# Softmax probabilities divided at the attention output, the table add fused with the row maximum, and the output projection's weight splits moved to GpSimd

## The chip, the cores and the metric

The kernel runs on one core of one Trainium2 chip. Five engines work in parallel, each through its own queue in order: TensorE (PE in the profile, with its weight loads shown apart as PEld), VectorE (DVE), ScalarE (ACT), GpSimd (POOL) and SyncE (SP), which here issues every transfer between the chip's memory (HBM) and the on-chip buffer (SBUF). TensorE writes only into PSUM, eight banks of 128 x 512 float32. The metric is the device time of one execution in microseconds (us); lower is better.

## The reference, cut to what matters

The program is two layers of a diffusion backbone over 256 latent tokens of width 1024, with 256 context tokens beside them in the first layer. Each layer is a half-step feed-forward, a mixer, and a second half-step feed-forward, each followed by a layer norm. The mixer of layer 0 is the neighbourhood attention that the change touches: 16 heads of 64, each latent query sees the latent keys in a window of 16 columns (a position table is added to these scores, and masked keys get minus infinity) and all 256 context keys, in one softmax.

```python
s_win = jnp.einsum('bjqhd,bjkhd->bhjqk', q_r, k_blk).astype(jnp.float32) * scale
s_win = jnp.where(mask, s_win + bias.astype(jnp.float32)[None], -jnp.inf)
s_ctx = jnp.einsum('bjqhd,bchd->bhjqc', q_r, k_c).astype(jnp.float32) * scale
p = jax.nn.softmax(jnp.concatenate([s_win, s_ctx], axis=-1), axis=-1).astype(v.dtype)
return (jnp.einsum('bhjqk,bjkhd->bjqhd', p[..., :nk], v_blk)
        + jnp.einsum('bhjqc,bchd->bjqhd', p[..., nk:], v_c))
...
y_lat = jnp.moveaxis(o, 0, 1).reshape(B, S, D) @ w_out
```

All matrices are float32, and the products have to keep nearly float32 precision.

## The kernel before, in words

**Precision.** TensorE multiplies in a rounded float32 type. Every operand x is therefore split into hi (x rounded, made by ACT with a copy) and lo (x minus hi, made by DVE with a subtraction), and each product is three matmuls: hi by hi, hi by lo, lo by hi (function `mmu`, lines 156, 157 and 159). Weights go through `wunit`: SP loads a unit of 128 x 1024 into one of four raw buffers, ACT makes hi (line 178), DVE makes lo (line 181). Activations go through `split` (lines 105 and 106).

**Order.** TensorE's instructions stand in the order in which the Python code issues them. For the other engines a scheduler chooses the order by priority; `tc.high_priority(offset=n)` lets what stands under it go ahead of the n instructions issued before it. For weight units n is `W_EARLY` = 40.

**The attention stage** is one loop over 32 steps. A step is one head h and one half qt of the 256 queries (128 queries), in the order (h,0), (h+1,0), (h,1), (h+1,1), so that two steps share a pair of heads. What one turn i of the loop issues:

- in even turns, `scores` for steps i and i+1: six matmuls into two PSUM banks S (128 queries x 512 keys: 256 latent, then 256 context; line 814). Then for each bank DVE adds the table to the 256 latent scores (818) and takes the negated row maximum over all 512 (820), ACT takes exp with that as bias and sums the row (822), DVE inverts the sum (823), and ACT multiplies the row by the inverse (824). The result is the tile pr.
- `bias_pair` for the pair of steps two turns ahead: SP gathers the table for each head from HBM, POOL adds the window mask (line 730). The table comes reversed within each grid row of 64 keys, and line 818 reads it backwards.
- `probs_T` for step i-2: four TensorE transposes of pr into a PSUM bank (line 836), then a split into pT (hi by ACT, lo by DVE).
- `values` for a head whose second half is done, one turn later: eight matmuls with v (lines 848 and 849) into a bank, then ACT and DVE (854, 855) add the two halves of the bank into `osum`, which holds two heads, and after the odd head `split` turns `osum` into oT, the operand of the output projection.
- between these, `fill_some` issues fillers: groups of six 512-column matmuls of the coming q, k and v projections (wkv, wq) and, from turn 24 on, of the output projection (wo, in `last_filler`). How many a turn gets is set by the table `rate` (R0 to R3). From turn 24 on it is one a turn, until nine are out; the other seven follow the loop.

Transposes of k (kT, line 773), of q and of pr share two PSUM banks (tag "tp"), so each waits until ACT and DVE have split what the bank held before. After the stage follow the layer norm and the second feed-forward.

## Time and profile before

| quantity | value |
|---|---|
| median of 3 runs | 1286.15 us (1283.31 to 1291.49) |
| the profiled execution: own time | 1289.17 us |
| its span, first to last instruction | 1287.4 us |
| instructions | 17193 |
| TensorE busy | 1257.7 us (98%) |
| VectorE busy | 955.1 us (74%) |
| ScalarE busy | 591.2 us (46%) |
| GpSimd busy | 42.0 us (3%) |
| mean granted TensorE clock | 0.996 |
| HBM traffic | 268.59 MB, mean 209 GB/s |

The durations that follow all come from the one profiled execution. A row of a group names the line, the engine, the operation, output and inputs, the shape and the count; behind the bar stand the total busy time, the mean of one in ns, and how long the engine stood idle just before, with what ended the idleness. TensorE's matmuls are pipelined and their ends are modelled: a 512-column matmul is shown with 390 ns, but the next one starts 227 ns later, so a busy TensorE can hold small gaps.

### The profile page before, as it was taken

What the parts mean: (1) busy time and instruction counts of PE and PEld (TensorE: products, weight loads), DVE (VectorE), ACT (ScalarE), POOL (GpSimd) and SP (SyncE); (2) the same over time, 40 slices, a digit from 0 to 9 for tenths busy, and PEclk for the clock granted to TensorE, in tenths of its full rate; (3) what the DMA queues carried; (4) which work ended last, traced back from release to release, by engine and by line L of the source; (5) the groups of instructions that cost most, each with busy time, mean ns of one, the idle gap of its engine ahead of it and who ended that gap; (6) DMA issues with size and microseconds to landing.
All of it is one profiled execution on the core that took longest, in us unless ns stands there. A gap on an engine that the chain in (4) does not pass through costs nothing.

```text
span 1287.4 us, 17193 instructions
## 1 busy us (share of the span) xinstructions
PE 1257.7 (98%) x5890; PEld 1007.0 (78%) x5890; DVE 955.1 (74%) x1683; ACT 591.2 (46%) x1148; POOL 42.0 (3%) x71
## 2 busy tenths in 40 slices
PE   7999999999999999988999999999999999999997
PEld 4787778788778877766887787887787877788886
DVE  3699877485658777788998787757778788855545
ACT  2432132413236456686555435654435645655431
POOL 0000000000001111110000000000000000000000
PEclk9999999999999999999999999999999999999999
DMA  9977569484622744464999887666887764666641
GB/s 284 299 231 243 181 193 297 131 297 146 198 78 76 215 91 92 90 147 149 305 331 328 295 294 262 215 215 225 289 287 241 215 211 147 210 217 185 231 155 51
DMA packets 202712, 268.59 MB, mean 209 GB/s; under 512 B 30026, under 2 KB 149298, under 8 KB 202624
## 3 DMA queue, kind: packets, MB, share of 16 engines
q1 hardware_dynamic: 202624, 267.49, 65.9%
q8 instruction: 46, 0.75, 0.2%
q14 instruction: 42, 0.34, 0.1%
HBM read 265.27 MB, written 2.17 MB: 208 GB/s over the span
## 4 chain that ended last, share of the span: by engine, by line
PE 78%; DVE 8%; DMA 8%; ACT 3%; issue 2%; SPq 1%; POOL 0%; DVEq 0%; ACTq 0%
PE w L156 13%; PE w L157 13%; PE w L159 13%; PE f L541 6%; PE f L542 6%; PE f L543 6%; DMA ar<-in_ada_w_dram 5%; DMA w1r<-in_ffn_w_in_dram 2%; PE wkv L156 2%; PE wkv L157 2%; PE wkv L159 2%; PE wc L156 2%; PE wc L157 2%; PE wc L159 2%; DVE w1l L181 2%
## 5 line engine op out<-in xcount | busy, mean ns | idle before, releaser
L178 ACT ACTIVATE w1h<-w1r 128x512 fp32r<-128x512 f32 x352 | 203.3, 626 | 185.0 <-PE w L159 75.4
L181 DVE TENSOR_TENSOR w1l<-w1r,w1h 128x512 fp32r<-128x512 f32 x352 | 227.6, 684 | 66.5 <-ACT w1h L178 64.3
L156 PE MATMUL w<-w1h,hTh 128*128 128x512 f32 x528 | 211.6, 401 | 3.8 <-ACT hTh L105 3.7
L247 DVE SCALAR_TENSOR_TENSOR acc<-ar,cst,acc 128x512 f32<-128x512 f32 x266 | 187.2, 745 | 34.8 <-DMA ar<-in_ada_w_dram 34.8
L157 PE MATMUL w<-w1l,hTh 128*128 128x512 f32 x528 | 207.7, 393 | 0.0
L156 PE MATMUL w<-w2h,gh 128*128 128x512 f32 (+1 forms) x446 | 175.4, 394 | 0.0
L157 PE MATMUL w<-w2l,gh 128*128 128x512 f32 (+1 forms) x446 | 173.7, 390 | 0.3 <-DVE w2l L181 0.3
L178 ACT ACTIVATE w2h<-w2r 128x512 fp32r<-128x512 f32 x176 | 101.5, 624 | 140.9 <-PE w L159 131.6
L159 PE MATMUL w<-w1h,hTl 128*128 128x512 f32 x528 | 163.9, 392 | 0.6 <-DVE hTl L106 0.6
L181 DVE TENSOR_TENSOR w2l<-w2r,w2h 128x512 fp32r<-128x512 f32 x176 | 114.0, 686 | 43.5 <-ACT w2h L178 42.3
L541 PE MATMUL f<-h0h,w1h 128*128 128x512 f32 x352 | 139.8, 397 | 0.4 <-ACT w1h L178 0.4
L542 PE MATMUL f<-h0h,w1l 128*128 128x512 f32 x352 | 138.4, 393 | 0.0
L543 PE MATMUL f<-h0l,w1h 128*128 128x512 f32 x352 | 138.3, 393 | 0.0
L159 PE MATMUL w<-w2h,gl 128*128 128x512 f32 (+1 forms) x446 | 136.3, 387 | 0.0
L156 PEld LDWEIGHTS w<-w1h,hTh 128*128 128x128 f32 x528 | 99.5, 188 | 28.2 <-ACT hTh L105 5.5
L159 PEld LDWEIGHTS w<-w1h,hTl 128*128 128x128 f32 x528 | 99.5, 189 | 24.1 <-DVE hTl L106 1.4
L157 PEld LDWEIGHTS w<-w1l,hTh 128*128 128x128 f32 x528 | 99.6, 189 | 20.4 <-DVE w1l L181 0.3
L156 PEld LDWEIGHTS w<-w2h,gh 128*128 128x128 f32 x446 | 83.7, 188 | 21.7 <-issue 1.7
L157 PEld LDWEIGHTS w<-w2l,gh 128*128 128x128 f32 x446 | 83.8, 188 | 18.6 <-DVE w2l L181 1.3
L159 PEld LDWEIGHTS w<-w2h,gl 128*128 128x128 f32 x446 | 83.3, 188 | 18.7
L541 PEld LDWEIGHTS f<-h0h,w1h 128*128 128x128 f32 x352 | 66.6, 189 | 18.4 <-issue 3.7
L543 PEld LDWEIGHTS f<-h0l,w1h 128*128 128x128 f32 x352 | 66.5, 189 | 14.7 <-DVE h0l L519 0.3
(178 smaller groups left out, 1702.5 us busy)
## 6 DMA issues: line engine op xcount, KB each, us to landing
w1r<-in_ffn_w_in_dram SPq DMA_DIRECT2D x352, 256.0 KB
ar<-in_ada_w_dram SPq DMA_DIRECT2D x128, 512.0 KB
w2r<-in_ffn_w_out_dram SPq DMA_DIRECT2D x88, 512.0 KB
ar<-in_ada_w_dram SPq DMA_DIRECT2D x32, 256.0 KB
wkvr<-in_na_w_qkv_dram SPq DMA_DIRECT2D x32, 256.0 KB
wcr<-in_sc_w_in_dram SPq DMA_DIRECT2D x32, 256.0 KB
wqr<-in_na_w_qkv_dram SPq DMA_DIRECT2D x8, 512.0 KB
bias<-in_na_rpb_dram SPq DMA_DIRECT2D x64, 64.0 KB
```

Source lines behind the costliest of these rows:

```text
L156: nc.tensor.matmul(ps, lh, rh, start=first and i == 0, stop=False)
L157: nc.tensor.matmul(ps, lh, rl, start=False, stop=False)
L159: nc.tensor.matmul(ps, ll, rh, start=False, stop=last and i == n - 1)
L178: nc.scalar.activation(hi[:, a:a + m // W_HI], raw[:, a:a + m // W_HI], AF.Copy)
L181: nc.vector.tensor_tensor(out=lo[:, a:b], in0=raw[:, a:b], in1=hi[:, a:b].bitcast(F32), op=ALU.subtract)
L247: nc.vector.scalar_tensor_tensor(out=a, in0=src, scalar=sc, in1=a, op0=ALU.mult, op1=ALU.add)
L541: nc.tensor.matmul(ps, lh, hT0[k][0], start=(k == 0), stop=False)
L542: nc.tensor.matmul(ps, ll, hT0[k][0], start=False, stop=False)
L543: nc.tensor.matmul(ps, lh, hT0[k][1], start=False, stop=(k == KC - 1))
```

## The change

Seven edits, all but one in the attention stage:

1. The table add, the maximum over 512 keys and the negation become one DVE instruction, `tensor_tensor_reduce`. It writes S = -(S + table) and the row minimum of that; exp is taken of -S. The table tile now has five slots of 256 columns; the slot in the middle is zero, and each head's operand is its own slot followed by the zero slot, so that all 512 keys can be read as one operand.
2. The reversal of the table moves: k is transposed and split into reversed order within each 64 keys (function `back`), and ACT writes exp back in normal order.
3. The probabilities are no longer divided (the ACT multiplication of line 824 goes). DVE writes the inverse of the row sum 64 times over (128 x 128 for a pair of heads), TensorE transposes that into the free half of the odd head's output bank (two transposes for each pair of heads), and DVE multiplies `osum` by it before the split.
4. In `last_filler`, a flag `calm` changes `wunit`: hi is one ACT instruction of 1024 columns, lo is made by POOL in two of 512, and both get a priority lead of `CALM` = 10 in place of 40. The load keeps its lead of 40.
5. The rate of turns 24 to 31 falls from 1.0 to `R4` = 0.75; turns 32 and on have 1.0. So six fillers go out by turn 31, and one each in turns 32, 33 and 34.
6. The k scratch tiles of 256 columns have five buffers in place of eight.
7. Two small tiles at the start and in the convolution stage (crow, srow) share the two buffers of another small tile (mrow) in place of having their own.

```diff
+CALM = 10
+R4 = 0.75
...
         with tc.high_priority(offset=w_early[0]):
             for src, c in srcs:
                 sync.dma_start(rv[:, :, c:c + src.shape[2]], src)
-            m = kn * 512
+        m = kn * 512
+        if calm[0]:
+            with tc.high_priority(offset=CALM):
+                nc.scalar.activation(hi[:, :m], raw[:, :m], AF.Copy)
+                for a in range(0, m, 512):
+                    nc.gpsimd.tensor_tensor(out=lo[:, a:a + 512], in0=raw[:, a:a + 512],
+                                            in1=hi[:, a:a + 512].bitcast(F32), op=ALU.subtract)
+            return hv, lv
+        with tc.high_priority(offset=w_early[0]):
...
-    crow = cp.tile([16, P], F32, tag="crow", name="crow")
+    crow = sp.tile([32, P], F32, tag="mrow", bufs=2, name="crow")[0:16]
...
-            return hp.tile([P, n], F32, tag="kr", bufs=8, name=nm("kr"))
+            return hp.tile([P, n], F32, tag="kr", bufs=5, name=nm("kr"))
...
+    def back(t):
+
+        return t.rearrange("p (a b) -> p a b", b=64)[:, :, ::-1]
...
+        if not bz:
+            bz.append(hp.tile([P, 5, 4, 64], F32, tag="bias", name="bias"))
+            nc.gpsimd.memset(bz[0][:, 2], 0.0)
         for hh in (h, h + 1):
-            bt = hp.tile([P, 4, 64], F32, tag="bias", bufs=4, name=nm("bias"))
+            n = 3 * qt + hh % 2
+            bt = bz[0][:, n]
...
-            BIAS[hh, qt] = bt[:, :, ::-1]
+            BIAS[hh, qt] = bass.AP(bz[0].tensor, bt.offset, [bt.ap[0], [(2 - n) * 256, 2], [1, 256]])
...
-                split(ps, hi, lo)
+                split(ps.rearrange("p (a b) -> p a b", b=64), back(hi), back(lo))
                 kT.append((hi, lo))
...
+        mx = hp.tile([P, 4 + P], F32, tag="mx", bufs=5, name=nm("mx"))
         for i, S in enumerate(banks):
-            Sv = S[:, 0:256].rearrange("p (a b) -> p a b", a=4)
-            nc.vector.tensor_tensor(out=Sv, in0=Sv, in1=BIAS.pop((h + i, qt)), op=ALU.add)
-            mx = hp.tile([P, 3], F32, tag="mx", bufs=6, name=nm("mx"))
-            nc.vector.tensor_reduce(out=mx[:, 0:1], in_=S, axis=AX.X, op=ALU.max, negate=True)
+            Sv = S.rearrange("p (c n) -> p c n", c=2)
+            nc.vector.tensor_tensor_reduce(out=Sv, in0=Sv, in1=BIAS.pop((h + i, qt)), scale=-1.0, scalar=3.0e38,
+                                           op0=ALU.add, op1=ALU.min, accum_out=mx[:, i:i + 1])
             pr = hp.tile([P, 512], F32, tag="pr", bufs=4, name=nm("pr"))
-            nc.scalar.activation(pr, S, AF.Exp, bias=mx[:, 0:1], accum_out=mx[:, 1:2])
-            nc.vector.reciprocal(mx[:, 2:3], mx[:, 1:2])
-            nc.scalar.activation(pr, pr, AF.Copy, scale=mx[:, 2:3])
+            nc.scalar.activation(back(pr), S.rearrange("p (a b) -> p a b", b=64), AF.Exp, bias=mx[:, i:i + 1], scale=-1.0,
+                                 accum_out=mx[:, 2 + i:3 + i])
             res.append(pr)
+        nc.vector.reciprocal(mx[:, 4:].rearrange("p (i d) -> p i d", i=2), mx[:, 2:4].unsqueeze(2).to_broadcast([P, 2, 64]))
+        RS[h, qt] = mx[:, 4:]
...
-        ps = mmb("o")[:, 0:256]
+        bk = mmb("o")
+        ps = bk[:, 0:256]
+        if h % 2:
+            for qt in range(2):
+                nc.tensor.transpose(bk[:, 256 + qt * P:256 + (qt + 1) * P], RS.pop((h - 1, qt)), ident)
...
+            nc.vector.tensor_tensor(out=osum[0], in0=osum[0], in1=bk[:, 256:512], op=ALU.mult)
             split(osum[0], *(z[:, cs] for z in oT[h // 4]))
...
     def last_filler():
+        calm[0] = True
...
-    rate = [R0] * 8 + [R1] * 8 + [R2] * 8 + [R3] * 12
+    rate = [R0] * 8 + [R1] * 8 + [R2] * 8 + [R4] * 8 + [R3] * 4
...
     run(fill)
     run(fin)
+    calm[0] = False
...
-    srow = cp.tile([24, P], F32, tag="srow", name="srow")
+    srow = sp.tile([32, P], F32, tag="mrow", bufs=2, name="srow")[0:24]
```

What this does to the order of instructions shows best at three places. The first is the end of the attention loop on TensorE, its last two `probs_T` and what follows. Before, the last filler ends, and the transposes of the last two probability tiles (PT) stand back to back with the value products (o) of the last even head right behind them:

```order
L159 MATMUL wo_5288<-woh_5357,oT_5036 128x512 x2
L836 MATMUL PT_5423<-ident,pr_5338 128x128 x4
L836 MATMUL PT_5430<-ident,pr_5345 128x128 x4
L848 MATMUL o_5437<-pT_5370,v_4682 128x256
L849 MATMUL o_5437<-pT_5371,v_4682 128x256
```

In the change the same place on TensorE has a filler of six matmuls between the two, and the product starts behind the second:

```order
L858 MATMUL PT_5293<-ident,pr_5225 128x128 x4
L159 MATMUL wo_5131<-woh_5301,oT_4953 128x512
L160 MATMUL wo_5131<-wol_5302,oT_4953 128x512
L159 MATMUL wo_5131<-woh_5301,oT_4953 128x512
L160 MATMUL wo_5131<-wol_5302,oT_4953 128x512
L162 MATMUL wo_5131<-woh_5301,oT_4954 128x512 x2
L858 MATMUL PT_5313<-ident,pr_5228 128x128 x4
L875 MATMUL o_5320<-pT_5231,v_4624 128x256
L876 MATMUL o_5320<-pT_5232,v_4624 128x256
```

A second such filler now stands between the last even and the last odd head, and behind it, ahead of the odd head's eight products, the two transposes of the inverses (mx):

```order
L160 MATMUL wo_5189<-wol_5282,oT_4953 128x512
L162 MATMUL wo_5189<-woh_5281,oT_4954 128x512 x2
L871 MATMUL o_5338<-ident,mx_5155 128x128
L871 MATMUL o_5338<-ident,mx_5223 128x128
L875 MATMUL o_5338<-pT_5264,v_4624 128x256
```

So three of the nine fillers that the loop hands out have moved from turns 24 to 31 into its last three turns.

The second place is DVE's queue in the last third of the loop, from one pair of steps to the next. Before, it holds for each pair two adds, two reductions, two reciprocals, two pT splits, one `osum` add per head, and the output projection's lo parts (wol):

```order
L181 TENSOR_TENSOR wol_5358<-wor_5356,woh_5357 128x512
L106 TENSOR_TENSOR pT_5016<-PT_5128,pT_5015 128x4x128
L823 RECIPROCAL mx_5075<-mx_5075 128x1
L820 TENSOR_REDUCE mx_5082<-S_5067 128x1
L106 TENSOR_TENSOR pT_5040<-PT_5149,pT_5039 128x4x128
L181 TENSOR_TENSOR wol_5358<-wor_5356,woh_5357 128x512
L855 TENSOR_TENSOR osum_5165<-o_5156,osum_5165 64x256
L823 RECIPROCAL mx_5082<-mx_5082 128x1
L818 TENSOR_TENSOR S_5168<-S_5168,bias_5088 128x256
L818 TENSOR_TENSOR S_5169<-S_5169,bias_5092 128x256
L820 TENSOR_REDUCE mx_5177<-S_5168 128x1
L820 TENSOR_REDUCE mx_5184<-S_5169 128x1
```

In the change a pair of steps on DVE reads as follows (ISA is the fused instruction, each followed by a 128x1 readout of its minimum):

```order
L839 ISA S_5077,mx_5085<-S_5077,bias 128x512
L839 ISA mx_5085 128x1
L839 ISA S_5078,mx_5085<-S_5078,bias 128x512
L839 ISA mx_5085 128x1
L109 TENSOR_TENSOR pT_5100<-PT_5101,pT_5099 128x4x128
L845 RECIPROCAL mx_5085<-mx_5085 128x128
L882 TENSOR_TENSOR osum_5074<-o_5108,osum_5074 64x256
L888 TENSOR_TENSOR osum_5074<-osum_5074,o_5108 128x256
L109 TENSOR_TENSOR pT_5139<-PT_5140,pT_5138 128x4x128
L109 TENSOR_TENSOR oT_4954<-osum_5074,oT_4953 128x256
```

The lo parts are gone from it, one reciprocal of 128 columns stands for two of one, and the multiplication of `osum` (line 888) stands ahead of the split.

The third place is POOL's queue, which before held nothing but the mask adds in this stage. In the change the lo parts stand between them from the tenth pair of steps on:

```order
L750 TENSOR_TENSOR bias<-bias,wmask 128x256 x18
L184 TENSOR_TENSOR wol_5026<-wor_5024,woh_5025 128x512 x2
L750 TENSOR_TENSOR bias<-bias,wmask 128x256 x4
L184 TENSOR_TENSOR wol_5047<-wor_5045,woh_5046 128x512 x2
L750 TENSOR_TENSOR bias<-bias,wmask 128x256
L184 TENSOR_TENSOR wol_5126<-wor_5124,woh_5125 128x512 x2
L750 TENSOR_TENSOR bias<-bias,wmask 128x256
L184 TENSOR_TENSOR wol_5171<-wor_5169,woh_5170 128x512 x2
L184 TENSOR_TENSOR wol_5282<-wor_5280,woh_5281 128x512 x2
L750 TENSOR_TENSOR bias<-bias,wmask 128x256 x8
```

The mask adds of the twelfth and thirteenth pair now stand behind lo parts, which wait for ACT's hi; six more lo parts follow the last mask add.

More of the change, by code (lines that the diff above doesn't have):

```diff
@@ L84, in backbone_kernel @@
     w_early = [0]
+    calm = [False]
     ext = [1, 0]
@@ L718, in backbone_kernel @@
     BIAS = {}
+    bz = []
+    def back(t):
+        return t.rearrange("p (a b) -> p a b", b=64)[:, :, ::-1]
     def bias_pair(h, qt):
+        if not bz:
+            bz.append(hp.tile([P, 5, 4, 64], F32, tag="bias", name="bias"))
+            nc.gpsimd.memset(bz[0][:, 2], 0.0)
         for hh in (h, h + 1):
-            bt = hp.tile([P, 4, 64], F32, tag="bias", bufs=4, name=nm("bias"))
+            n = 3 * qt + hh % 2
+            bt = bz[0][:, n]
             for i in range(2):
@@ L815, in scores @@
         res = []
+        mx = hp.tile([P, 4 + P], F32, tag="mx", bufs=5, name=nm("mx"))
         for i, S in enumerate(banks):
[L817 to L820 removed]
+            Sv = S.rearrange("p (c n) -> p c n", c=2)
+            nc.vector.tensor_tensor_reduce(out=Sv, in0=Sv, in1=BIAS.pop((h + i, qt)), scale=-1.0, scalar=3.0e38,
+                                           op0=ALU.add, op1=ALU.min, accum_out=mx[:, i:i + 1])
             pr = hp.tile([P, 512], F32, tag="pr", bufs=4, name=nm("pr"))
[L822 to L824 removed]
+            nc.scalar.activation(back(pr), S.rearrange("p (a b) -> p a b", b=64), AF.Exp, bias=mx[:, i:i + 1], scale=-1.0,
+                                 accum_out=mx[:, 2 + i:3 + i])
             res.append(pr)
+        nc.vector.reciprocal(mx[:, 4:].rearrange("p (i d) -> p i d", i=2), mx[:, 2:4].unsqueeze(2).to_broadcast([P, 2, 64]))
+        RS[h, qt] = mx[:, 4:]
         return res
     PT = {}
+    RS = {}
     def probs_T(h, qt, pr):
```

## The prediction, as it was made before the run

> **What bounds the kernel now.** I read the page first, for the engine that fills the span.
>
> ```profile
> span 1287.4 us, 17193 instructions
> PE 1257.7 (98%) x5890; PEld 1007.0 (78%) x5890; DVE 955.1 (74%) x1683; ACT 591.2 (46%) x1148; POOL 42.0 (3%) x71
> ```
>
> TensorE does, with 98%, and the change takes no matmul from it. It can only win back the 2% in which TensorE stands, and only where it acts. So next came the busy time by stretches of the attention stage (columns: stretch, length, then PE, PEld, DVE, ACT and POOL, granted clock, DMA share, GB/s).
>
> ```profile
> 440.00:540.00 100.00, 99.68 (x521) 78.76 (x520) 74.44 (x161) 59.77 (x130) 14.08 (x18) 1.00 0.48 105
> 540.00:566.00 26.00, 22.74 (x130) 17.13 (x129) 21.91 (x46) 22.10 (x49) 5.38 (x6) 0.93 0.61 131
> 566.00:592.00 26.00, 22.71 (x133) 18.00 (x132) 19.25 (x45) 19.32 (x43) 3.08 (x4) 1.00 0.50 125
> 557.60:561.20 3.60, 3.60 (x12) 2.36 (x11) 3.60 (x7) 1.35 (x3) 1.05 (x3) 0.53 0.46 65
> ```
>
> For 100 us TensorE is full, whatever DVE and ACT do. Only in the last 50 us, where fillers run thin, does it stand: 3.26 us and 3.29 us. The last row, a part of the second, has the clock at half for 3.4 us, which costs 1.7 us more. The view of waits says for what PE stood, first in 540 to 566, then in 566 to 592 (total, times, longest):
>
> ```profile
> PE kT L773 <- DVE pT L106: 2.0, 2, 1.5
> PE o L848 <- ACT pT L105: 0.7, 1, 0.7
> PE o L849 <- DVE pT L106: 0.6, 1, 0.6
> ...
> PE o L849 <- DVE pT L106: 0.9, 2, 0.5
> PE o L848 <- DVE osum L855: 0.9, 1, 0.9
> PE wo L156 <- ACT oT L105: 0.9, 1, 0.9
> PE PT L836 <- DVE pT L106: 0.5, 1, 0.5
> ```
>
> They add up to 6.5 us: nearly all are waits for the split of the transposed probabilities. With the clock, about 8 us is all that this change can return.
>
> **The change part by part.** The prices come from the groups of instructions of the loop, 440 to 592 (behind the count the busy time and the mean ns of one, then the idle time before them and what ended it); the last row is the view of one tile, with shortest, median and longest.
>
> ```profile
> L824 ACT ACTIVATE pr<-pr,mx 128x512 f32<-128x512 f32 x32 | 22.6, 726 | 0.5 <-DVE mx L823 0.5
> L730 POOL TENSOR_TENSOR bias<-bias,wmask 128x256 f32<-128x256 f32 x28 | 22.5, 809 | 124.6 <-DMA bias<-in_na_rpb_dram 94.3 <-DVE oT L106 19.4 <-DVE pT L106 7.6
> L106 DVE TENSOR_TENSOR pT<-PT,pT 128x512 fp32r<-128x512 f32 x32 | 21.9, 687 | 11.9 <-ACT pT L105 11.4
> L105 ACT ACTIVATE pT<-PT 128x512 fp32r<-128x512 f32 x32 | 18.9, 595 | 11.3 <-PE PT L836 11.2
> L820 DVE TENSOR_REDUCE mx<-S 128x1 f32<-128x512 f32 x32 | 20.7, 677 | 0.1
> L818 DVE TENSOR_TENSOR S<-S,bias 128x256 f32<-128x256 f32 x32 | 12.6, 422 | 4.2 <-PE S L814 3.2 <-issue 0.6
> L181 DVE TENSOR_TENSOR wol<-wor,woh 128x512 fp32r<-128x512 f32 x16 | 10.9, 687 | 0.9 <-ACT woh L178 0.9
> L855 DVE TENSOR_TENSOR osum<-o,osum 64x256 f32<-64x256 f32 x16 | 6.6, 416 | 4.8 <-ACT osum L854 4.6
> L823 DVE RECIPROCAL mx<-mx 128x1 f32<-128x1 f32 x32 | 5.1, 158 | 4.9 <-ACT pr L822 4.8
> L106 DVE TENSOR_TENSOR v<-wkv,v 128x256 fp32r<-128x256 f32 x13 | 5.4, 418 | 2.3 <-ACT v L105 2.3
> L713 DVE TENSOR_TENSOR r<-wkv,rope 128x128 f32<-128x128 f32 x12 | 2.9, 280 | 0.0
> L181 DVE TENSOR_TENSOR wkvl<-wkvr,wkvh x32: 641/683/1249, 406.7 to 517.7; 128x512 fp32r<-128x512 f32 x32
> ```
>
> *Transposes of the inverses.* Sixteen more on TensorE, the full engine, so they cost what they last. Four transposes in TensorE's timeline:
>
> ```profile
> 481.82 0.60 PE L836 MATMUL PT<-ident,pr 128*128 128x128 f32 x4
> 482.18 0.48 PE L156 MATMUL wkv<-wkvh,hTh 128*128 128x512 f32 x1
> ```
>
> From start to next start the four take 0.36 us, 0.09 each; the filler behind them starts slowly (0.48 where 0.39 is usual), which I count as 0.09 for each pair of heads. So 0.18 to 0.27 for each of eight pairs, 1.4 to 2.2 us. I take **+2.0**.
>
> *ACT* loses 32 x 726 ns = 23 us, nothing that PE feels before 540, where it is full.
>
> *DVE, for two steps.* Out go 2 x (422 + 677 + 158) ns = 2.51 us. In come two fused instructions and one reciprocal of 128 columns; the trace shows neither. A fused one handles 512 columns with one operand from PSUM, like the pT split: 0.69 us is the nearest row; at most I give it 1.25, the longest wkvl row. The reciprocal: 0.28 as the 128-column row L713, from 0.16 (L823) to 1.25. A readout of the minimum may follow each fused one, 0.16 as L823. I take 2 x 0.69 + 0.28 + 2 x 0.16 = 1.98 us. The osum multiplication adds 0.42 (L855; 0.28 to 0.69) to every second pair of steps. The lo parts, 10.9 us, go to POOL. Reading backwards costs nothing in the table add: 422 ns against 418 for the plain 256-column split of v; I count the reversed k splits and exp at nothing too, since PE is full beside most of them, and at most 0.2 us in each of the five last pairs.
>
> For the reciprocal the Trainium skill has a rule against the change: in "VectorE: DVE Perf Modes", section "First, the fixed hardware budget", it divides iteratively with a repeat count of 8. If every column paid eight cycles of 1.04 ns (the rows of 512 and of 256 columns differ by that much a column), my estimate from that page would be 1.1 us for 128 columns, and two steps on DVE would grow by 0.8 us; the sum below would stay, and the room that DVE has in the last turns would be gone. No run here shows it; the 158 ns of one column cannot.
>
> *The stretch without fillers, 546 to 557.* PE waits in a latency chain, of which these are the end:
>
> ```profile
> 553.22 0.28 PE L849 MATMUL o<-pT,v 128*128 128x256 f32 x1
> 553.34 0.60 PE L836 MATMUL PT<-ident,pr 128*128 128x128 f32 x4
> 555.19 0.59 ACT L105 ACTIVATE pT<-PT 128x512 fp32r<-128x512 f32 x1
> 556.55 0.66 PE L773 MATMUL kT<-ident,kr 128*128 128x128 f32 x4 [1.55 <-DVE pT L106]
> 557.14 0.50 PE L814 MATMUL S<-kTh,qTh 64*128 64x512 f32 x2
> ```
>
> The transposes end at 553.94; ACT takes them up 1.25 us later, because multiplications and hi parts stand ahead in its full queue. ACT idles 3.9 us in 540 to 566, of which 2.25 in the stretch of the half clock, behind this chain. Two multiplications for a pair of steps (1.45 us) go, and the hi parts get a lead of 10 in place of 40. That gives at least the 1.25; the DVE lo part gone from the same place gives up to 0.69 more. A hi part is now one instruction of 1024 columns, by L105 some 1.2 us, and where one slips ahead of a pT hi it costs that chain up to 0.6 more than before; the smaller lead makes it rarer. With two banks for all transposes the rest of the chain, split by split, stays, and so do the two o waits. I take the scores to come 1.8 us earlier: **-1.8** (bounds 0 and -3.3, the three waits).
>
> Whether the half clock goes, too, is open. Between the matmuls of 553.22 and 557.14 that are no transposes lie 3.70 us, behind which it began; 1.9 would be left, 2.1 if the new transposes lie in it. The trace's other case:
>
> ```profile
> 796.09 0.61 PE L159 MATMUL w<-w2h,gl 128*128 128x512 f32 x2
> 799.41 0.50 PE L156 MATMUL w<-w1h,hTh 128*128 128x512 f32 x1 [2.71 <-ACT hTh L105]
> 800.10:803.60 3.50, 3.50 (x10) 2.70 (x9) 3.40 (x7) 3.41 (x7) 0.04 (x1) 0.52 0.10 34
> ```
>
> There an idle of 2.71 us sufficed. What is left may fall on either side; I leave the 1.7 us where they are and keep them in the range. The Trainium skill, in "TensorE: Matmul & The Clock Gate", Part 1, wants an idle window of about 3.4 us. By that -1.7 us would be added to the sum; the 2.71 us of this trace speak against it.
>
> *Turns 24 to 34.* Three fillers of six matmuls move to where PE stood. Matmuls follow each other here:
>
> ```profile
> 480.68 0.39 PE L157 MATMUL wkv<-wkvl,hTh 128*128 128x512 f32 x1
> 480.91 0.39 PE L156 MATMUL wkv<-wkvh,hTh 128*128 128x512 f32 x1
> 564.54 0.50 PE L814 MATMUL S<-kTh,qTh 64*128 64x512 f32 x2
> 570.26 0.49 PE L814 MATMUL S<-kTh,qTh 64*128 64x512 f32 x2
> ```
>
> 0.23 us each, so a filler covers 1.36 us, more than any wait of 566 to 592. Those for osum (0.9), the last PT (0.5) and pT (0.9) are covered: 2.3 us, and 0.1 refilling behind each of four (0.38 for the first product where 0.28 is usual), -2.7. The wait for oT behind the last head stays and gets the multiplication, 0.42 us, and up to 0.1 of queueing: +0.5. Sum **-2.2**. In turns 24 to 31 two fillers are missing, 2.7 us in four pairs of steps; a pair, 5.72 us from scores to scores in the two rows above, has 5.1 with the new transposes. DVE's share of it is 1.98 + 2 x 0.69 + 0.42 + half of a multiplication and of an oT split (0.42) = 4.2 us, so it fits.
>
> *POOL and the queues.* Sixteen lo parts of 512 columns: twice the 809 ns of L730, 1.6 us each (bounds 0.8 and 2.0). They start behind ACT's hi, and in POOL's queue the mask adds of the twelfth and thirteenth pair of steps stand behind some of them. Mask adds waited 94.3 us for their transfers, so most have room; those of the twelfth pair, which the fused instruction needs right behind the filler-free stretch, have the least, within 1 us of need by my count. The fused instruction stands in DVE's queue ahead of pT splits, so a late mask add delays those and, behind them, the products: 0 in the sum, 2 to 4 as a rival. SP's loads of wo wait until POOL gives back one of four raw buffers, and the table loads and the next stage's weights are queued behind them on SP; I take 0, as DMA had a share of 0.50 in 566 to 592, and keep the 1.6 us of one lo part as the other end. Where POOL runs, DVE operations on two operands from SBUF got slower (the wkvl row has 641 at best and 1249 at worst); of these the last turns hold only oT's split and the osum multiplication's neighbours, some 0.2 us each off the path but for the last, inside the 0.5 above. kr, crow and srow: their buffers' waits lie under a full PE, 0, at most one 256-column operation (0.42) where k is transposed last.
>
> **Sum**: +2.0 - 1.8 - 2.2 = -2.0, against the profiled execution's 1289.17: 1287.2. That execution lies 3.0 above the median 1286.15, inside the spread of the three runs, so I forecast **1284** us.
>
> **The rivals.** *Latency, not load*: the chain split by split keeps its waits though ACT is emptier, for in the rows of pT DVE idled 11.4 us waiting for ACT's hi, and ACT 11.2 us waiting for PE's transposes, so neither was late by its load there. Only +2.0 and the 0.5 remain: 1288.7, 20%. Against it: the chain at 553 to 557, where ACT took the transposes up 1.25 us late. *All goes*: every wait covered and the clock full, 2.0 - 3.3 - 3.2 - 0.8 (refilling, eight times 0.1) - 1.7 = -7.0: 1279. For it speaks that ACT was full at the stretch; against it the two banks; 17%. *POOL late*: the mask add behind the lo parts holds DVE for 2 to 4 us, half of which PE's fillers cover: 1286, 8%. *DVE the bound, slower*: if the fused instruction and the reciprocal both take 1.25 us, DVE's pair of steps is 4.2 + 2 x 0.56 + 0.97 = 6.3 us, above PE's 5.1, for four pairs: +4.8. The relieved waits then stay, +2.0 and +0.5 beside them: +7.3, 1293.5. It decides from the point where fused pair and reciprocal exceed the 1.66 us taken by 0.9. For it: no row shows either instruction, and fewer fillers mean less cover; against it: each 512-column DVE row with a PSUM operand is near 0.68; 10%. *The lead doesn't reach*: with a lead of 10 the hi and lo parts of the last fillers come so late that the products which were to cover the waits wait themselves, for wol on POOL. Then the 2.2 of the last turns are not had: 2.0 - 1.8 = +0.2, 1286.4. For it: two lo parts in a row last 3.2 us on POOL where DVE took 1.37; against it: the moved fillers have been issued a turn or more, over 5 us, ahead. 10%. My forecast has 35%.
>
> **Range and chances.** The run to run spread of 8 us (1283 to 1291) and the unknown prices: the range 1274 to 1294 holds all but the fringe of the second rival (5%), the upper half of the DVE rival (5%) and what I haven't thought of (5%). About 1% (13 us) is what a measurement of this kernel can tell from no change. Faster by more needs all waits and more: 5%. Slower by more: a part of the DVE rival with prices above 1.25, POOL's tail, and the unforeseen: 9%. Within: 86%.
>
> **What would show it.** Right: the waits of kT and PT below 1.0 us in sum, osum gone from the waits, the oT wait at 1.4, PE idle in 540 to 592 at 3 us or less, fused instructions near 0.69 and reciprocals near 0.28 us. Half clock again near 556: that term as taken; none: the 1.7 goes. Wrong: DVE with no idle time between 560 and 590; new waits for mx, for bias on DVE, or for wol at the last fillers.

## The result, and the profile after

The changed kernel takes 1292.3 us (median of 22 runs, 1288.46 to 1295.27) against 1287.25 us before (22 runs, 1283.07 to 1291.49): ratio 1.0042, 95% interval 1.0033 to 1.0051. It is 5 us slower. The forecast was 1284, 2 us faster; the time lies inside the stated range, but on the other side. The prediction took 1% as the least that can be told from no change; with 22 runs of each kernel it is 0.1%.

The spans of the two profiled executions don't show this: after, 1286.7 us (own time 1288.46, the fastest of its 22 runs); before, 1287.4 us (1289.17, above its median). So I compare by stage. These rows of the views of two tiles, first of before, then of after, give the first and the last start of a pair's first score matmuls (S) and of the transposes (gT) in the feed-forward behind the attention:

```profile
L814 PE MATMUL S<-kTh,qTh x32: 491/496/502, 441.8 to 576.7; 64*128 64x512 f32 x32
L400 PE MATMUL gT<-ident,sil x132: 270/272/328, 623.1 to 1222.5; 128*128 128x128 f32 x132
```

```profile
L834 PE MATMUL S<-kTh,qTh x32: 492/497/792, 441.1 to 580.1; 64*128 64x512 f32 x32
L411 PE MATMUL gT<-ident,sil x132: 270/272/275, 627.7 to 1222.1; 128*128 128x128 f32 x132
```

From the first scores to the first gT it was 181.3 us and is 186.6: 5.3 us more, the whole difference. Nearly all of it lies between the scores behind the stretch without fillers (before at 557.14, now at 555.73) and the last ones, 19.57 us before and 24.33 now. These are the rows of the two stretches, with the engines as in the prediction's table (the last three numbers are the granted clock, the DMA share and GB/s):

```profile
557.14:576.71 19.57, 19.07 (x103) 14.58 (x102) 15.57 (x35) 13.99 (x32) 5.24 (x7) 0.91 0.71 174
555.73:580.06 24.33, 20.02 (x100) 15.29 (x99) 14.35 (x29) 10.47 (x24) 6.84 (x9) 0.86 0.66 129
```

Of the 4.8 us more, 1.6 are the lower clock (0.14 of 24.33 against 0.09 of 19.57), and TensorE's idle time grew from 0.5 to 4.3 us, with one filler less in the stretch. Behind the first gT the profile of after is 5.0 us shorter again (gT to gT, 594.4 against 599.4), for the larger part because that one execution had neither the wait nor the half clock that before had near 800 us (last row below). Further stretches of after, three of them as they were shown of before:

```profile
440.00:540.00 100.00, 99.83 (x526) 79.10 (x524) 72.10 (x152) 50.05 (x112) 16.02 (x20) 1.00 0.46 102
540.00:566.00 26.00, 20.30 (x120) 15.49 (x119) 17.16 (x34) 16.57 (x35) 13.96 (x14) 0.97 0.59 130
566.00:592.00 26.00, 24.72 (x135) 19.40 (x134) 18.32 (x36) 13.20 (x29) 8.46 (x9) 0.90 0.46 105
564.00:572.00 8.00, 7.34 (x31) 6.06 (x31) 4.57 (x10) 2.94 (x8) 0.72 (x1) 0.57 0.75 198
...
796.00:806.00 10.00, 9.08 (x44) 7.16 (x43) 8.23 (x15) 7.59 (x18) 0.68 (x2) 1.00 0.71 237
```

In 540 to 566 TensorE now stands 5.70 us where it stood 3.26, though ScalarE has fallen from 22.10 to 16.57 us and DVE from 21.91 to 17.16. The half clock (the row from 564) lasts 6.8 us where it was 3.4. What TensorE waits for in 540 to 597:

```profile
PE o L875 <- ACT pT L108: 3.3, 2, 2.9
PE o L876 <- DVE pT L109: 1.7, 3, 0.7
PE wo L159 <- ACT oT L108: 1.4, 1, 1.4
PE kT L793 <- DVE pT L109: 1.4, 1, 1.4
PE PT L858 <- DVE pT L109: 0.5, 1, 0.5
```

The wait for osum is gone, that for oT is 1.4 as forecast, and kT's has shrunk from 2.0 to 1.4. One wait of 2.9 us is new, for ACT's pT. It leads back through five engines. In this order, the next rows come from the timelines of SP, POOL, DVE, ACT and TensorE:

```profile
544.68 0.37 SPq L178 DMA_DIRECT2D wor<-in_na_w_out_dram  x1
548.31 3.55 SPq L178 DMA_DIRECT2D wor<-in_na_w_out_dram  x2
551.95 3.23 SPq L746 DMA_DIRECT2D bias<-in_na_rpb_dram  x4
...
548.93 5.02 POOL L184 TENSOR_TENSOR wol<-wor,woh 128x512 fp32r<-128x512 f32 x4
560.21 1.41 POOL L750 TENSOR_TENSOR bias<-bias,wmask 128x256 f32<-128x256 f32 x2 [6.26 <-DMA bias<-in_na_rpb_dram]
...
560.96 0.70 DVE L839 CUSTOM_DVE_ANT_1 S<-S,bias 128x512 f32<-128x512 f32 x1 [3.44 <-POOL bias L750]
...
561.75 0.69 ACT L842 ACTIVATE pr<-S,mx 128x512 f32<-128x512 f32 x1 [4.72 <-DVE mx L839]
563.17 1.07 ACT L108 ACTIVATE pT<-PT 128x512 fp32r<-128x512 f32 x2
...
563.82 0.38 PE L875 MATMUL o<-pT,v 128*128 128x256 f32 x1 [2.90 <-ACT pT L108]
```

SP issues three loads of wo, each when POOL gives a raw buffer back; then the table of the thirteenth pair of steps. Before, that table was issued ahead of the second of these loads; its rows there, on SP and on POOL:

```profile
547.50 2.61 SPq L726 DMA_DIRECT2D bias<-in_na_rpb_dram  x4
553.40 0.73 POOL L730 TENSOR_TENSOR bias<-bias,wmask 128x256 f32<-128x256 f32 x1 [6.27 <-DMA bias<-in_na_rpb_dram]
```

So it is issued 4.5 us later, and from the issue to the mask add it takes 8.3 us where it took 5.9, behind three loads of 0.5 MB each. POOL stands idle for 6.26 us until then: its lo parts are out of the way by 554. DVE waits 3.44 us for the table. ACT has the two exps of these scores in its queue ahead of the pT splits, and stands 4.72 us, in the end with two transposed banks before it, one transposed at 558.49 and one at 560.32. TensorE has used up its fillers and stands.

The prices of what the trace of before could not show, from the groups of after, 440 to 597:

```profile
L839 DVE CUSTOM_DVE_ANT_1 S<-S,bias 128x512 f32<-128x512 f32 x24 | 16.3, 706 | 8.7 <-PE S L834 4.5 <-POOL bias L750 3.4 <-issue 0.6
L839 DVE DVE_READ_ACCUMULATOR2_ANT mx<- 128x1 f32 x32 | 4.5, 141 | 0.0
L845 DVE RECIPROCAL mx<-mx 128x128 f32<-128x128 f32 x16 | 15.2, 951 | 10.5 <-ACT pr L842 10.5
L888 DVE TENSOR_TENSOR osum<-osum,o 128x256 f32<-128x256 f32 x8 | 3.3, 418 | 0.2
L184 POOL TENSOR_TENSOR wol<-wor,woh 128x512 fp32r<-128x512 f32 x16 | 20.2, 1288 | 12.9 <-ACT woh L182 12.9
```

The fused instruction (706 ns), its readout (141) and the multiplication (418) lie near the values taken; POOL's lo part took 1.29 us where 1.6 were taken, inside its bounds. The reciprocal is far off: 951 ns where 280 were taken.

### The profile page after: what moved, and what is told of

Its sections match the earlier page's. It is cut to its first block, busy times and chain, and to the rows that moved or that the text cites. A ratio compares the mean times of both kernels' runs of the same rounds, so it can differ in the third digit from the quotient of the medians.

```text
span 1286.7 us, 17207 instructions
## 1 busy us (share of the span) xinstructions
PE 1258.1 (98%) x5906; PEld 1007.9 (78%) x5906; DVE 951.4 (74%) x1659; ACT 572.8 (45%) x1108; POOL 60.3 (5%) x88
## 4 chain that ended last, share of the span: by engine, by line
PE 90%; DVE 4%; DMA 3%; ACT 1%; issue 1%; POOL 0%; SPq 0%; DVEq 0%; ACTq 0%; POOLq 0%
PE w L159 17%; PE w L160 17%; PE w L162 17%; PE f L552 6%; PE f L554 6%; PE f L553 6%; PE wkv L159 2%; PE wkv L160 2%; PE wkv L162 2%; DMA ar<-in_ada_w_dram 2%; PE wc L159 2%; PE wc L160 2%; PE wc L162 2%; PE gT L411 1%; PE S L834 1%; PE ada L276 1%
## 5 line engine op out<-in xcount | busy, mean ns | idle before, releaser
L552 PEld LDWEIGHTS f<-h0h,w1h 128*128 128x128 f32 x352 | 66.4, 189 | 17.8 <-issue 4.1
```

What stands on the lines that cost most here:

```text
L552: nc.tensor.matmul(ps, lh, hT0[k][0], start=(k == 0), stop=False)
```

## The experiments

Each kernel was timed in five rounds against the kernel before; the ratio is to that kernel, with its 95% interval. One thousandth is 1.3 us.

**The theory, and its rivals.** Late table: with the lo parts on POOL a third wo load stands ahead of a table load on SP, and what that table then delays makes the 5 us. Slow VectorE: the long reciprocal and the sixteen transposes make them. Thin fillers: the lower rate of fillers in turns 24 to 31 makes them.

**Lo parts back on VectorE**, all other edits kept:

```diff
-                    nc.gpsimd.tensor_tensor(out=lo[:, a:a + 512], in0=raw[:, a:a + 512],
+                    nc.vector.tensor_tensor(out=lo[:, a:a + 512], in0=raw[:, a:a + 512],
```

> The changed kernel with one line turned back: the lo parts of the output projection are made by VectorE, in two of 512 columns; the lead of 10 and all other edits stay. Late table (the wo loads wait on SP for GpSimd's 1.29 us lo parts, the table of the pair at 561 us is queued behind them, and the fused instruction waits 3.4 us for it): that wait falls below 0.5 us, the half clock near 564 us is at most 3.4 us long, and the time is 4 to 6 us below the changed kernel's, 1286 to 1288. Slow VectorE (reciprocal of 0.95 us and 16 transposes): VectorE gets 11 us more work, the time stays at 1292 or rises to 1295. Thin fillers (two fewer in turns 24 to 31): 1292, unchanged.

Measured: 1286.68 us, 0.9995 (0.9981 to 1.0008). All 5 us are gone, and the wait for a table does not occur. SP's timeline now has the table (the first bias row) ahead of the third load:

```profile
544.02 2.15 SPq L178 DMA_DIRECT2D wor<-in_na_w_out_dram  x2
548.50 2.62 SPq L746 DMA_DIRECT2D bias<-in_na_rpb_dram  x4
551.26 0.51 SPq L178 DMA_DIRECT2D wor<-in_na_w_out_dram  x1
553.62 2.61 SPq L746 DMA_DIRECT2D bias<-in_na_rpb_dram  x4
```

The pace differs, too: two loads go out within 2.15 us, where with lo on POOL three took 7.2. SP's waits for a raw buffer in 530 to 600 were 16.2 us for POOL and 10.7 for ACT in the changed kernel, and are 19.1 us for VectorE here. Whether the place or the pace counts more, this run does not separate. What follows is that the lo parts on POOL make the 5 us, and neither rival does: both expected 1292 or more.

**The fourth edit taken back whole** (also two hi parts, lead 40): the line `calm[0] = True` left out.

> The changed kernel without its fourth edit: hi in two of 512 columns on ScalarE, lo on VectorE, both with a lead of 40, as before; fusion, division and rate stay. Late table: as with lo on VectorE, 1286 to 1288; a difference of over 1.5 us between the two would be the price of the lead. Slow VectorE: 1292 to 1295. Thin fillers: 1292.

Measured: 1287.85 us, 1.0000 (0.9987 to 1.0012). Against the run with lo on VectorE, the lead and the single hi part make no difference that this can tell.

**Six table slots**, POOL's lo parts kept. The table is there earlier by a pair of steps, and nothing else is meant to move:

(kr and mx have four buffers each, to make room.)

```diff
-            bz.append(hp.tile([P, 5, 4, 64], F32, tag="bias", name="bias"))
+            bz.append(hp.tile([P, 7, 4, 64], F32, tag="bias", name="bias"))
-            n = 3 * qt + hh % 2
+            n = (h + qt) % 3 * 2 + hh % 2
+            n += n > 2
```

> The changed kernel with GpSimd's lo parts, lead and rate as they are, but six table slots in place of four, so that a pair's table is loaded one pair of steps earlier (kr and mx have one buffer fewer to make room). Late table: the fused instruction's wait for the table at 561 us falls below 0.5 us though nothing else changes, and the time is 3 to 6 us below the changed kernel's, 1286 to 1289. Slow VectorE or thin fillers: 1292, unchanged. If GpSimd's lo parts themselves are late for the products: new waits of TensorE for wol, and 1291 or more.

Measured: 1288.01 us, 1.0006 (0.9993 to 1.0018), with this left of DVE's wait for POOL's table:

```profile
DVE S L840 <- POOL bias L751: 0.5, 1, 0.5
```

That is the case for the table itself. SP still issues the three wo loads one behind the other, from 544.86 to 552.05, and still waits for POOL and ACT to give the buffers back (18.9 and 4.7 us where it was 16.2 and 10.7). Only the table of these scores is loaded earlier, and 4.6 of the 5 us are gone (0.0036 of 1287). From the scores behind the stretch without fillers to the last ones it takes 17.7 us where the change took 24.3, and the clock stays full there.

**The edits one at a time, on the kernel before**, each with the lines that the diff above shows for it. The fourth alone (`calm`):

> The kernel before with the fourth edit alone: lo parts on GpSimd, hi in one, lead of 10; no fusion, no moved division, rate 1.0. Late table: GpSimd's queue again has lo parts between the two adds of one pair of steps, so the add on VectorE waits 1 to 4 us for the table, and the time is 1288 to 1292 against 1287 before. Slow VectorE or thin fillers: 1286 to 1287.5, as before or a little below, as VectorE has 11 us less.

Measured: 1289.31 us, 1.0016 (1.0003 to 1.0029). The third alone, the division, with kr at five buffers:

> The kernel before with the third edit alone (division at the output: 128-column reciprocals, 16 transposes, multiplication of osum; kr with five buffers to make room); table add and maximum apart, lo parts on VectorE, rate 1.0. Price of the division: 16 transposes at 0.09 to 0.13 us on a full TensorE (+1.4 to +2.2), the multiplication in the last wait for oT (+0.5), against the ACT multiplications' share of the waits (0 to -1.8): 1286.5 to 1289.5. If ScalarE was what held the stretch without fillers, below 1286.

Measured: 1290.64 us, 1.0031 (1.0017 to 1.0045): above my expectation. The fusion and the reversal (first and second) alone:

> The changed kernel with the first and second edit alone (fused table add and minimum, reversed k, exp written backwards) and the small tiles as there; division on ScalarE, lo parts on VectorE with a lead of 40, rate 1.0. TensorE gets nothing, VectorE loses 0.26 us a score bank: 1285 to 1287, as the waits hang on the split of pT, behind fewer VectorE instructions. If the reversed forms or the fused one cost TensorE something, above 1288.

Measured: 1286.16 us, 0.9992 (0.9979 to 1.0005), as expected; its profile has 0.9 us of waiting for a table. The lower rate alone:

```diff
-    rate = [R0] * 8 + [R1] * 8 + [R2] * 8 + [R3] * 12
+    rate = [R0] * 8 + [R1] * 8 + [R2] * 8 + [R4] * 8 + [R3] * 4
```

> The kernel before with the fifth edit alone (six fillers in turns 24 to 31, three in turns 32 to 34). By the step of the prediction (waits of 2.3 us covered, with refilling 2.7): 1283.5 to 1285, and the waits for osum and the last PT gone. If fewer fillers in turns 24 to 31 open as much as they close: 1286 to 1288.

Measured: 1287.65 us, 0.9999 (0.9987 to 1.0011). That is no gain, where the prediction had 2.2 us. And the changed kernel with only the rate put back (`R4 = 1.0`):

> The changed kernel with the rate of turns 24 to 31 put back to 1.0, GpSimd's lo parts kept. Late table: three wo loads still stand ahead of the late table on SP, so 3 us of waiting for it stay, and the time is 1290 to 1294. Thin fillers: the time falls to 1286 to 1288.

Measured: 1292.54 us (7 runs), 1.0040 (1.0026 to 1.0055): the rate is not what made it slow. DVE's waits for a table in the fourth alone, the division alone, the rate alone, and the change at rate 1.0:

```profile
DVE S L828 <- POOL bias L740: 3.2, 3, 1.6
```

```profile
DVE S L819 <- POOL bias L730: 3.1, 3, 2.6
```

```profile
DVE S L819 <- POOL bias L731: 3.0, 1, 3.0
```

```profile
DVE S L839 <- POOL bias L750: 5.1, 4, 2.4
```

The profile of the kernel before has no such row. So each of these edits, alone, makes a table late in its profiled execution: the tables come just in time before. That any small shift of SP's loads or of the scores is enough for that is what I read from it; the runs do not show which shift it was in each. A single edit's time is its own price and a late table's.

**Six table buffers under each**, to have the edits without it; the control first.

```diff
-            bt = hp.tile([P, 4, 64], F32, tag="bias", bufs=4, name=nm("bias"))
+            bt = hp.tile([P, 4, 64], F32, tag="bias", bufs=6, name=nm("bias"))
-            return hp.tile([P, n], F32, tag="kr", bufs=8, name=nm("kr"))
+            return hp.tile([P, n], F32, tag="kr", bufs=5, name=nm("kr"))
```

> The control: the kernel before with six table buffers and five of kr. It waits for no table, so both theories expect no difference, ratio 0.9990 to 1.0010. Slower would be the price of the kr buffers, to be taken off the three others; faster, a late table in other executions than the one profiled.

Measured: 1288.08 us, 1.0013 (0.9996 to 1.0030). The six buffers may not be free, though the interval has room for no difference: in the control's profile the first scores wait for k, and half clock follows. That profile is of the slowest of its 12 runs (1294.4 us). The likely cause is the same queue with the roles exchanged, by SP's timeline in the control:

```profile
426.44 2.13 SPq L726 DMA_DIRECT2D bias<-in_na_rpb_dram  x3
...
433.03 0.60 SPq L726 DMA_DIRECT2D bias<-in_na_rpb_dram  x1
433.73 0.57 SPq L175 DMA_DIRECT2D wkvr<-in_na_w_qkv_dram  x1
```

and by the view of waits:

```profile
PE S L814 <- ACT kTh L105: 1.8, 1, 1.8
```

An extra table stands ahead of the weights wkvr, which before were issued at 426.73. Its profile still has 1.0 us of waiting for a table, too.

> The kernel before with the division at the output and six table buffers (kr five, mx four, small tiles shared). Late table: the wait of 3.1 us goes, and of the 4.0 us that the division alone cost 1 to 2.5 are left, the 16 transposes and the longer oT wait: ratio 1.0008 to 1.0020. The division itself costs it all: ratio 1.0025 to 1.0040.

Measured: 1287.02 us, 0.9997 (0.9983 to 1.0012), and no wait for a table. The division with the table on time costs nothing that can be told, less than I expected; alone it was 1.0031, and the two intervals don't meet.

> The kernel before with GpSimd's lo parts, the lead of 10, and six table buffers (kr five). Late table: the 2.1 us that this edit alone cost go, ratio 0.9990 to 1.0005. If GpSimd's lo parts are late for the products themselves: 1.0012 or more, with TensorE or VectorE waiting for other things than a table.

Measured: 1288.03 us, 1.0005 (0.9988 to 1.0021), a wait of 0.8 us left. Lower than without, but inside the uncertainty.

> The kernel before with the lower rate of turns 24 to 31 and six table buffers (kr with five). Late table stands in for the rate: the wait of 3.0 us for a table is under 0.5 us, and the time is 1.5 to 3 us below before, ratio 0.9977 to 0.9988. The rate itself is worth nothing: ratio 0.9992 to 1.0005, as with four buffers.

Measured: 1286.63 us, 0.9998 (0.9981 to 1.0015). That is what was expected if the rate itself is worth nothing. Against the control it is 2 us better, but their intervals overlap, so it stays undecided by itself.

The traces agree with the late table in all three. From the scores behind the stretch without fillers to the last ones, the fourth edit, the division and the rate alone take 20.3, 21.4 and 20.6 us; with six buffers they take 17.6, 17.8 and 18.5; the half clock takes at most 1.8 of any of these.

**What the division is made of.** In the kernel with lo on VectorE, each transpose of the inverses issued twice:

```diff
+                for _ in range(2):
                     nc.tensor.transpose(bk[:, 256 + qt * P:256 + (qt + 1) * P], rs, ident)
```

> The kernel with lo on VectorE (no late table), and each of the 16 transposes of the inverses issued twice into the same place. The difference to that kernel (0.9995 of before) is the price of 16 transposes on TensorE. As the prediction has it, +1.4 to +2.2 us: 1288 to 1289, ratio 1.0006 to 1.0013. If they hide in TensorE's waits: no difference, 1286 to 1287.

Measured: 1289.05 us, 1.0012 (1.0001 to 1.0023), 2.2 us above the kernel that it was made from (0.9995), with intervals that overlap. That is near the price forecast for 16 transposes, but its profile also has 1.8 us of waiting for tables. In the traces, from the fourth to the eleventh pair's scores, where TensorE is full, eight second copies cost 0.54 us (72.30 against 71.76), so 1.1 for sixteen; the transposes' own part is likely that small.

And the reciprocal of two columns, spread over 128 by ScalarE:

```diff
-        nc.vector.reciprocal(mx[:, 4:].rearrange("p (i d) -> p i d", i=2), mx[:, 2:4].unsqueeze(2).to_broadcast([P, 2, 64]))
+        nc.vector.reciprocal(mx[:, 2:4], mx[:, 2:4])
+        nc.scalar.activation(mx[:, 4:].rearrange("p (i d) -> p i d", i=2), mx[:, 2:4].unsqueeze(2).to_broadcast([P, 2, 64]), AF.Copy)
```

> The kernel with lo on VectorE, and the reciprocal taken of two columns instead of 128; ScalarE, which has room, spreads it over 128 columns. VectorE loses some 0.8 us a pair of steps. If the reciprocal's 0.95 us in front of the pT splits is what took back the gain of the stretch without fillers (scores 0.65 us earlier, not 1.8): kT's wait falls from 1.4 us to 1.0 or less and the time by 0.5 to 1.5 us, to 1285.2 to 1286.2. If ScalarE's chain alone sets it: unchanged or up to 0.5 us longer.

Measured: 1287.22 us, 0.9995 (0.9981 to 1.0009), the same as without. The reciprocal takes 162 ns in place of 951 and kT's wait falls only from 1.4 to 1.2 us:

```profile
552.76 0.60 PE L859 MATMUL PT<-ident,pr 128*128 128x128 f32 x4
555.01 0.66 PE L793 MATMUL kT<-ident,kr 128*128 128x128 f32 x4 [1.18 <-DVE pT L109]
```

1.65 us lie between the end of the transposes (553.36) and kT: little more than one split, hi 0.60 and lo 0.69. Little gain is left in this chain as long as two banks hold all transposes; a third bank was not tried. My expectation of 0.5 to 1.5 us was wrong.

**Six slots with lo on VectorE:**

> The kernel with lo on VectorE and six table slots (kr and mx with one buffer fewer). There is no wait for a table left to remove, so by the late table 1286 to 1287.5, the same as with four slots. Below 1285 would mean that the table's place on SP also holds up the loads of the next stage.

Measured: 1288.84 us, 1.0013 (1.0000 to 1.0025). This is not faster, and above my expectation. The price of the slots, as in the control, would explain it: its first scores wait 1.2 us for k. The intervals here and with four slots overlap, so it is not shown.

**Without the division.** Fusion and lower rate, six slots, lo on VectorE:

> Fusion, reversed k and the lower rate with six table slots; no division at the output (ScalarE multiplies as before), lo on VectorE with a lead of 40. If the division's transposes, reciprocal and multiplication are what takes back the gain of the other edits, and the tables are on time: 1283 to 1285.5, faster than both kernels, with the waits for osum and the last PT gone. If the lower rate opens other waits: 1286 to 1288, and what PE waits for says which.

Measured: 1285.07 us, 0.9981 (0.9967 to 0.9996): 2.4 us faster than before, where the change is 5 us slower. TensorE's waits in 540 to 597:

```profile
PE o L872 <- DVE pT L109: 2.0, 2, 1.7
PE wo L159 <- ACT oT L108: 1.5, 1, 1.5
PE kT L794 <- DVE pT L109: 1.0, 1, 1.0
PE S L835 <- DVE kTl L109: 0.2, 1, 0.2
```

Osum, PT and ACT's pT are gone from the list, as the prediction's step on the rate had it; the 1.7 us wait for DVE's pT is in the list of the fusion alone, too. Two more kernels complete the square of rate and slots:

> Fusion and reversed k with six table slots, rate 1.0, no division at the output, lo on VectorE. If the lower rate is worth the predicted 2.2 us when the tables are on time, this kernel is 1.5 to 2.5 us slower than the one with the lower rate: ratio 0.9992 to 1.0003, with the wait for osum (0.9) back. If the gain is that of the table alone: 0.9978 to 0.9987.

> Fusion, reversed k and the lower rate with four table slots, no division at the output, lo on VectorE. If a late table eats what the rate gives, as with the rate alone: ratio 0.9990 to 1.0000 and a wait of VectorE for a table over 2 us. If the rate gives it without more slots: 0.9978 to 0.9987 and no such wait.

Measured, six slots at rate 1.0: 1287.6 us, 1.0004 (0.9991 to 1.0018), with osum's 0.9 us back. The lower rate with four slots: 1284.47 us (11 runs), 0.9990 (0.9978 to 1.0001), with 1.2 us of waiting for tables, less than a late table was expected to show. With six slots the rate is worth 1.0004 - 0.9981 = 0.0023, 3.0 us, with four (0.9992 - 0.9990) 0.3. The intervals within each pair overlap, so this speaks for the predicted 2.2 us where the tables are on time, but does not show it. The traces say less: from the scores behind the stretch without fillers to the first gT the lower rate saves 1.1 us in each pair (64.6 to 63.5 with four slots, 64.8 to 63.7 with six), and in the second pair the slower kernel has a half clock of some 1.7 us there.

## Why the prediction was wrong

**The step that failed** is the one on POOL and the queues: "I take 0, as DMA had a share of 0.50". It weighed the wo loads' wait by the load of the DMA engines. What counted was SP's queue: three loads that wait for buffers from POOL, ahead of a table that the next scores need. DVE waited 3.4 us for that table, and behind the long idle of TensorE the half clock lasted 3.4 us longer, which costs some 1.7. In the trace the three pairs of steps behind it took 4.8 us more. The runs agree in size: 4.6 us came back with six slots, and 6.0 (1.0042 - 0.9995) with lo on VectorE. The mean granted clock fits, too: 0.9951 in the 22 runs against 0.9962 in the 158 of the kernel before beside the experiments, and 0.0011 x 1290 = 1.4 us by this estimate. "Within 1 us of need by my count" was right on how little room there was: before, the second mask add of the pair behind the filler-free stretch ended at 557.62, its scores at 558.63. It is the thirteenth pair, not the twelfth, and the point should have had more weight than 8%.

Of the 8.3 us between forecast and measurement, about 1.1 is no fault of a step: the three runs that the forecast started from had a median 1.1 us below that of the 22.

**The rival POOL late** named the mechanism, a late mask add that holds DVE for 2 to 4 us, and DVE did wait 3.44. It had the path and the sum wrong: POOL was idle when the table came, SP and the transfer were late; and it let fillers cover half, where TensorE had none left. With the 4.8 us of the trace in place of 2 it gives 1289.

**DVE the bound** did not happen: the fused instruction took 0.71 us, and DVE stood idle for 8.8 of 26 us in 540 to 566. The reciprocal took 0.95, though, far from the 0.28 of the row that I took as nearest. That row was of another operation: alike in shape only. The Trainium skill ("VectorE: DVE Perf Modes", "First, the fixed hardware budget") says that it divides iteratively with a repeat count of 8; the estimate of 1.1 us that the prediction worked out from this was near the trace's 0.95. The time did not feel it by more than the uncertainty, as the run with the cheap reciprocal shows.

**Term by term, with the table on time:**
- Transposes +2.0: of the right size or a little high. The doubled ones put them at 2.2 by the times, with the reservations made there; the traces put them lower. From the fourth to the eleventh pair's scores it was 70.96 us before and is 71.80, with eight transposes more: 0.1 us each, 1.7 for sixteen.
- The stretch without fillers -1.8: over-sized. ACT's lateness fell from 1.25 to 0.25 us (transposes end at 553.19, ACT's split starts at 553.44), but what is late next stood right behind it, on DVE, where the reciprocal (553.59 to 554.54) held the lo part. From the end of the transposes to kT it was 2.6 us and is 1.95. From the scores two pairs earlier to those behind the stretch it was 12.3 us (544.86 to 557.14); it is 11.2 in the change (544.50 to 555.73) and 11.7 with lo on VectorE (545.09 to 556.80), each with two of the new transposes in it. So the stretch gave some 0.6 to 1.3 us, the upper end with 0.2 added for the two.
- Turns 24 to 34, -2.2: the wait for osum went and oT's became 1.4, both as stated; the one for PT (0.5) stayed. The square above puts the rate's gain at 0.3 to 3.0 us, with an uncertainty as large, and the traces there at 1.1 or less. With lo on VectorE the gain is not to be seen: from the scores behind the stretch to the first gT it takes 66.7 us where before took 65.9, six transposes included, with as much half clock in both; oT's wait is 2.2 us there, and one of 1.0 for kT's lo part is new.
- DVE's fewer instructions were worth little, as forecast: fusion alone 0.9992. For ACT's 23 us there is only the division with six buffers, 0.9997 with its transposes, which shows no gain.

So with lo on VectorE the edits give 0.9995, which is 0.6 us where -2.0 was forecast. The 1.4 us between lie inside the interval (0.9981 to 1.0008); the traces, one execution each, put what is missing into the stretch and the last turns, and how much into each stays open.

**The clock.** The prediction left the half clock where it was. In the profile of after it did not come there: behind the 3.0 us without matmuls (transposes not counted) ahead of 555.73 the clock stayed full, and the half clock followed the 3.3 us ahead of 563.82, the wait that the table made. The Trainium skill ("TensorE: Matmul & The Clock Gate", Part 1) says that half clock follows an idle window of about 3.4 us, and that the window runs freely and does not start with the kernel. That it runs freely fits the scatter shown below; the length does not agree with the 2.71 us that sufficed before.

## What to carry to other kernels

Moving work to an idle engine changes when its input buffers come free, and with them the order in which one transfer queue serves everything else. Before counting such a move as free, list what stands on that queue behind the loads that now wait longer or come earlier, and how long each can be late: here a table with about 1 us of room. And measure an edit together with the wait that it may cause: alone, the division seemed to cost 4 us (1.0031), and with the table on time nothing that could be told (0.9997).

## What was not expected of the hardware

A stretch of one length without matmuls (transposes not counted) brings the half clock in one execution and not in another. In the profile of before 3.64 us (553.50 to 557.14; the prediction has 3.70) were followed by it. In the kernel with the rate alone the last product and the next scores are as far apart (552.25 to 555.89), and the clock stays full:

```profile
551.97 0.28 PE L850 MATMUL o<-pT,v 128*128 128x256 f32 x1
555.89 0.50 PE L815 MATMUL S<-kTh,qTh 64*128 64x512 f32 x2
...
556.00:562.00 6.00, 6.00 (x36) 4.58 (x36) 5.94 (x13) 4.04 (x8) 2.27 (x3) 1.00 0.60 144
```

The runs of one kernel spread accordingly: the change's 22 runs average 1294.9 us at a mean clock of 0.993 (2 runs), 1292.5 at 0.995 (8) and 1289.5 at 0.997 (3). So one execution's profile can be 4 us off its median, nearly the size of the effect here, and when stage times are compared, what the clock took has to be told apart.

The reciprocal is dear by the column: 951 ns for 128 columns, 162 for two, so 6.3 ns a column, where the 512-column operations take 1.3 with their fixed part.
